# Last layer's experts: ranked by token count, sharing 128 columns in groups, with float32 weights unsplit

## The chip, the cores and the metric

The kernel runs on one core of a Trainium2 chip, as one launch. The metric is the time of one execution in device microseconds (us), median of the runs; less is better.

## The reference

Two transformer blocks in float32 run one after the other. The first block has two layers; each is a mixer (layer 0: Fourier mixing with neighbourhood attention; layer 1: retention) followed by a mixture of 16 experts of which each token takes two. Layer 0's experts see 512 tokens, layer 1's only the 256 latent tokens. The change touches the experts of layer 1 alone, whose weights are three matrices per expert: `w1` and `w3` of 1024x512, `w2` of 512x1024, 6 MB in float32 for each expert.

```python
def moe_ffn(tok, router_w, router_b, w1, w3, w2):
    T = tok.shape[0]
    scores = jax.nn.sigmoid((tok @ router_w).astype(jnp.float32))
...
    gate = jnp.sum(jax.nn.one_hot(expert_idx, N_EXPERTS, dtype=jnp.float32) * w[..., None], axis=1).astype(tok.dtype)
    out = jnp.zeros_like(tok)
    for e in range(N_EXPERTS):
        hid = jax.nn.silu(tok @ w1[e]) * (tok @ w3[e])
        out = out + gate[:, e:e + 1] * (hid @ w2[e])
    return out
```

With the reference's inputs, layer 1's 16 experts get 13, 23, 17, 17, 73, 64, 44, 39, 23, 20, 20, 17, 33, 45, 40 and 24 tokens (512 places in all).

## The kernel before

The residual stream `hT` lies transposed on the chip. The order of work is the program order of each engine's queue, set by the Tile framework's scheduler from the order in the code, from pools of buffers and from the semaphores that they need.

The function `moe(l, ss)` serves both layers. It routes (statistics, sigmoid, first two experts of the best group; `posm`, L1013, is each token's place in its expert's list), writes the tokens' normed rows into `nat` in a high and a low f32r part (L534, L537), and then works expert by expert, each in 128 columns:

- `choose` (L1050) makes one-hot columns for a pair of experts, `gather` (L1074) multiplies `nat` with them to get the transposed rows `xe` of the pair, read out on ScalarE and VectorE (L1079, L1077).
- `product` takes a weight in units of 1 MB. `unit` loads one (L172, issued on SP's queue into one of six 8 KB-per-partition buffers, four row blocks of 512 columns, so 2 KB in one piece), ScalarE rounds it to a high part `wh` (L186), VectorE, or GpSimd for every fourth block pair, makes the low part `wl` (L189). `mm3` (L198, L199, L200) then multiplies three times, high by high, low by high and high by low, 128 rows by 512 columns each. An expert has 24 such steps, layer 1 so 16x24x3 = 1152 matmuls.
- The hidden rows are transposed on TensorE (L258), split, and multiplied with `w2`; the result is scaled by the gate into `y` (L1099 ScalarE, L1100 VectorE), and `scatter` (L1119, L1120) adds the rows back through a one-hot `back` (L1103) into four PSUM banks `acc`, 16 matmuls for each expert.
- After expert 1, `overflow` holds a branch (L1217) for experts with more than 128 tokens, which is not taken. After expert 3, `bias_setup` prepares the second block's biases, with one large copy on GpSimd's queue.

After the last scatter `residual` adds the sum to `hT`, `stat_chunk2` (L473, L475) takes the squares, and `second` (L1311 on) is the second block, whose first products need the norm of the new stream.

## Time and profile before

| | us |
|---|---|
| median of 3 runs | 1856.89 |
| lowest and highest | 1853.49, 1857.39 |
| span of the profiled execution | 1851.5 |
| TensorE busy in the span | 1763.2 (95%) |
| layer 1's expert products, first to end of last | 1064.35 to 1404.18 |

The span is from the first to the last instruction in one execution under the profiler, the median is of whole executions; the profiled execution's own time outside the span is not given, so the difference of 5.4 us is taken as what lies around a span. In the second part of the page each digit is a fortieth of the span, 46.3 us; layer 1's experts are slices 23 to 30 (counted from 0).

### The profile page before, as it was taken

To read this page: it belongs to the slowest core of one execution; us is meant where nothing else is said; L and a number is where in the kernel's file an instruction comes from. 1 tells how busy PE (TensorE), PEld (TensorE's weight loads), DVE (VectorE), ACT (ScalarE), POOL (GpSimd) and SP (SyncE) were. 2 spreads that over 40 slices of the span, in tenths; PEclk is the share of its full clock that TensorE was granted. 3 is DMA by queue.
4 is the path that set the end of the run, shared out by engine and by line. 5 is a ranking of instruction groups with operands and counts; after the bars stand their busy time and mean duration, and the time that the engine had idled before them with its cause. 6 is when DMAs were issued, how large, how long until landed. Compare 5 with 4: busy or idle time off the path is not lost. (4 is left out here: it accounts for less than half of the span.)

```text
span 1851.5 us, 29457 instructions
## 1 busy us (share of the span) xinstructions
PE 1763.2 (95%) x11672; PEld 1500.9 (81%) x11672; DVE 1264.1 (68%) x1890; ACT 1002.0 (54%) x1388; POOL 492.7 (27%) x325
## 2 busy tenths in 40 slices
PE   6999999999999998999999899999998999999999
PEld 3766657777788876988999788888887989999989
DVE  6565553868888787654554587888887676577765
ACT  3343332656666665443343477777776455555543
POOL 2222102234444442220120243333333110122310
PEclk8999999999999998999999899999998999999999
DMA  9536544589888888355335279888885544543451
GB/s 315 140 111 198 185 144 182 199 277 293 283 284 290 293 290 301 115 205 183 117 113 194 80 262 332 294 307 309 291 285 159 166 143 152 188 133 119 137 190 39
DMA packets 249178, 384.13 MB, mean 207 GB/s; under 512 B 24273, under 2 KB 141074, under 8 KB 243850
## 3 DMA queue, kind: packets, MB, share of 16 engines
q1 hardware_dynamic: 245546, 373.71, 60.4%
q0 software_dynamic: 2608, 7.08, 1.9%
q8 instruction: 95, 1.56, 0.4%
q10 hardware_dynamic: 880, 1.38, 0.2%
q14 instruction: 49, 0.40, 0.1%
HBM read 375.19 MB, written 12.75 MB: 210 GB/s over the span
## 5 line engine op out<-in xcount | busy, mean ns | idle before, releaser
L189 DVE TENSOR_TENSOR wl<-w,wh 128x1024 fp32r<-128x1024 f32 x494 | 658.4, 1349 | 228.1 <-ACT wh L186 223.6
L186 ACT ACTIVATE wh<-w 128x1024 fp32r<-128x1024 f32 x592 | 621.5, 1059 | 343.4 <-PE ps L200 218.2
L189 POOL TENSOR_TENSOR wl<-w,wh 128x1024 fp32r<-128x1024 f32 x98 | 258.3, 2636 | 372.0 <-ACT wh L186 362.1
L199 PE MATMUL ps<-wl,xe 128*128 128x512 f32 x512 | 203.2, 397 | 13.5 <-POOL wl L189 13.0
L198 PE MATMUL ps<-wh,xe 128*128 128x512 f32 x512 | 203.7, 398 | 3.5 <-PEq L1217 3.5
L200 PE MATMUL ps<-wh,xe 128*128 128x512 f32 x512 | 201.8, 394 | 0.0
L198 PE MATMUL ps<-wh,xh 128*128 128x256 f32 x512 | 145.7, 285 | 1.1 <-DVE rt L799 0.7
L199 PE MATMUL ps<-wl,xh 128*128 128x256 f32 x512 | 143.7, 281 | 0.0
L200 PE MATMUL ps<-wh,xl 128*128 128x256 f32 x512 | 143.7, 281 | 0.0
L199 PEld LDWEIGHTS ps<-wl,xe 128*128 128x128 f32 x512 | 96.8, 189 | 39.7 <-POOL wl L189 20.1
L198 PEld LDWEIGHTS ps<-wh,xe 128*128 128x128 f32 x512 | 96.7, 189 | 23.6 <-issue 5.0
L200 PEld LDWEIGHTS ps<-wh,xe 128*128 128x128 f32 x512 | 96.6, 189 | 21.7 <-issue 0.8
L1074 PEld LDWEIGHTS ps<-oh,nat 128*128 128x128 f32 x768 | 104.3, 199 | 6.8 <-DVE oh L1050 1.2
L1074 PE MATMUL ps<-oh,nat 128*128 128x256 f32 x768 | 107.0, 291 | 0.8 <-DVE oh L1050 0.8
L199 PE MATMUL ps<-wl,hh 128*128 128x512 f32 x256 | 100.7, 393 | 2.2 <-DVE wl L189 2.2
L198 PE MATMUL ps<-wh,hh 128*128 128x512 f32 x256 | 101.0, 395 | 0.2 <-ACT xe L1079 0.2
L198 PE MATMUL ps<-x,wh 128*128 128x256 f32 x352 | 101.2, 288 | 0.0
L198 PEld LDWEIGHTS ps<-wh,xh 128*128 128x128 f32 x512 | 96.4, 188 | 5.4 <-issue 3.4
L200 PE MATMUL ps<-wh,hh 128*128 128x512 f32 x256 | 100.3, 392 | 0.0
L199 PE MATMUL ps<-x,wh 128*128 128x256 f32 x352 | 98.6, 280 | 0.0
L200 PE MATMUL ps<-x,wl 128*128 128x256 f32 x352 | 98.5, 280 | 0.0
L199 PEld LDWEIGHTS ps<-wl,xh 128*128 128x128 f32 x512 | 96.5, 188 | 0.1
(410 smaller groups left out, 4058.8 us busy)
## 6 DMA issues: line engine op xcount, KB each, us to landing
w<-in_moe_w_dram SPq DMA_DIRECT2D x192, 1024.0 KB, 6.0
w<-in_w_in_dram SPq DMA_DIRECT2D x48, 1024.0 KB, 5.5
w<-in_ada_w_dram SPq DMA_DIRECT2D x32, 1024.0 KB, 5.0
w<-in_ret_w_in_dram SPq DMA_DIRECT2D x24, 1024.0 KB, 5.4
w<-in_mixab_w_in_dram SPq DMA_DIRECT2D x10, 1024.0 KB, 6.0
w<-in_ada_w_dram SPq DMA_DIRECT2D x16, 512.0 KB, 8.8
ada<-in_ada_w_dram SPq DMA_DIRECT2D x8, 1024.0 KB, 9.0
w<-in_ret_w_out_dram SPq DMA_DIRECT2D x8, 1024.0 KB, 7.7
```

The lines of the kernel that those rows point to most:

```text
L186: nc.scalar.activation(hi, t[:, b:b + hk], AF.Copy)
L189: eng.tensor_tensor(out=lo, in0=t[:, b:b + hk], in1=hi.bitcast(F32), op=OP.subtract)
L198: mm(ps, lh, rh, start=start, stop=False, skip_group_check=skip)
L199: mm(ps, lh, rl, start=False, stop=False, skip_group_check=skip)
L200: mm(ps, ll, rh, start=False, stop=stop, skip_group_check=skip)
L1074: nc.tensor.matmul(ps[:, j], nat[part][:, t, k * P:(k + 1) * P], oh[:, t], start=t == 0, stop=t == NT - 1)
```

## The change

Layer 0 keeps `moe`, with its routing moved into `route`. Layer 1 gets `moe_late`. There, expert 15 is a group alone, and the other 15 are ranked by their token count on VectorE and GpSimd, after which they share 128 columns: the largest with one of the smallest, in nine groups (rank and columns below). The order of the ranks goes as integers to SP, which reads one before a group's loads and uses it in their addresses. A tile of 8 KB per partition holds 1 MB of a weight, now with 8 KB in one piece, since partition p takes rows 8p to 8p+7 (4p to 4p+3 in `w2`); `nat` and the hidden rows are written in the same spread order. The weights are multiplied as float32, unsplit, with float32 tokens; each expert's weights pass only the columns of its tokens: tiles of 32 columns in a group of 96 and 32, of 64 in a group of two 64s. Eight buffers for loads come on top of the standing three, in the room of the split weights' pool, which is released for the stage. The branch for overflow now tests whether any expert has more tokens than its columns.

```diff
+GROUPS = (((15, 128),), ((0, 96), (14, 32)), ((1, 96), (13, 32)), ((2, 64), (12, 64)), ((3, 64), (11, 64)),
+          ((4, 64), (10, 64)), ((5, 64), (9, 64)), ((6, 64), (8, 64)), ((7, 128),))
+CAPS = [dict(x for g in GROUPS for x in g)[r] for r in range(16)]
...
+            order = {}
+
+            def load(name, r, u, n, c):
+
+                w = I[name][l]
+                w = w[15:16] if r == 15 else w[bass.ds(order[r], 1)]
+                m = 2048 // c
+                return self.raw((P, m, c), w.rearrange("o (p k) c -> p (o k) c", k=n)[:, u * m:u * m + m, :])
+
+            def loads(g):
+
+                rs = [r for r, _ in GROUPS[g]]
+                return [[load(name, r, u, n, c) for r in rs]
+                        for name, n, c in (("moe_w1", 8, 512), ("moe_w3", 8, 512), ("moe_w2", 4, 1024)) for u in range(2)]
+
+            first = loads(0)
+            tl, places, gates, rows, nat = self.route(l, ss, rp, True)
...
+            b2 = lambda a, i: a.unsqueeze(i).to_broadcast([P, 16, 16])
+            key = tl([16])
+            V.scalar_tensor_tensor(out=key, in0=pos[:, 4, :], scalar=16.0, in1=self.down16, op0=OP.mult, op1=OP.add)
+            V.memset(key[:, 15:16], -1.0)
+            ge, up = tl([16, 16]), tl([16])
+            V.tensor_tensor(out=ge, in0=b2(key, 2), in1=b2(key, 1), op=OP.is_ge)
+            V.tensor_reduce(out=up, in_=ge, axis=AX.X, op=OP.add)
+
+            pm = tl([16, 16])
+            V.tensor_tensor(out=pm, in0=b2(up, 1), in1=b2(self.down16, 2), op=OP.is_equal)
+            V.tensor_tensor(out=ge, in0=pm, in1=b2(self.down16, 1), op=OP.mult)
+            V.tensor_reduce(out=up, in_=ge, axis=AX.X, op=OP.add)
+            oi = tl([16], I32, "order")
+            V.tensor_scalar(out=oi, in0=up, scalar1=-1.0, scalar2=16.0, op0=OP.mult, op1=OP.add)
+
+            def ranked(dst, x, eng):
+
+                t = tl([NT, 16, 16])
+                b4 = lambda a, i: a.unsqueeze(i).to_broadcast([P, NT, 16, 16])
+                eng.tensor_tensor(out=t, in0=b4(x, 2), in1=b4(pm, 1), op=OP.mult)
+                V.tensor_reduce(out=dst, in_=t, axis=AX.X, op=OP.add)
+
+            place = tl([NT, 16])
+            ranked(place, posm, V)
...
+            def choose(gs):
+
+                oh = wp.tile([P, NT, 256], F32R, tag="oh", name=self.name("oh"))
+                for t in range(NT):
+                    a = 0
+                    for g in gs:
+                        for r, n in GROUPS[g]:
+                            V.tensor_scalar(out=oh[:, t, a:a + n], in0=self.iota1[:, 0:n], scalar1=place[:, t, r:r + 1],
+                                            scalar2=None, op0=OP.is_equal)
+                            a += n
...
+            def gather(x, oh, w, c):
+
+                ps = self.psum((P, 2, 256))
+                for j in range(2):
+                    k = 2 * c + j
+                    for i in range(2 * NT):
+                        nc.tensor.matmul(ps[:, j, 0:w], nat[i % 2][:, i // 2, k * P:(k + 1) * P], oh[:, i // 2, 0:w],
+                                         start=i == 0, stop=i == 2 * NT - 1)
+                if c % 2:
+                    V.tensor_copy(x[:, 2 * c:2 * c + 2, 0:w], ps[:, :, 0:w])
+                else:
+                    nc.scalar.activation(x[:, 2 * c:2 * c + 2, 0:w], ps[:, :, 0:w], AF.Copy)
+
+            def columns(g):
+
+                ns = [n for _, n in GROUPS[g]]
+                w = min(min(ns), 128)
+                ends = np.cumsum(ns)
+                return [(a, a + w, int(np.searchsorted(ends, a, side="right"))) for a in range(0, P, w)]
+
+            def products(outs, lhs, ws, g):
+
+                m = ws[0][0].shape[1]
+                for u, we in enumerate(ws):
+                    for k in range(m):
+                        for c, ps in enumerate(outs):
+                            for a, b, e in columns(g):
+                                nc.tensor.matmul(ps[a:b], lhs(u * m + k)[:, a:b], we[e][:, k, 512 * c:512 * c + 512],
+                                                 start=u == k == 0, stop=u == len(ws) - 1 and k == m - 1)
+
+            def scatter(y, back, start, stop):
+                for k in range(KC):
+                    for i in range(2):
+                        nc.tensor.matmul(acc[k // 2][:, k % 2], y[i][:, k * P:(k + 1) * P], back,
+                                         start=start and k % 2 == i == 0, stop=stop and i == 1, skip_group_check=True)
+
+            def batch(gs):
+                oh, w = choose(gs)
+                return wp.tile([P, KC, 256], F32, tag="xe", name=self.name("xe")), oh, w
+
+
+            batches = [[0]] + [list(range(a, min(a + 2, NG))) for a in range(1, NG, 2)]
+            cur = batch(batches[0])
```

The loop over the groups, in the same order of steps as before, from the new file:

```diff
+            for bi, gs in enumerate(batches):
+                x, oh, _ = cur
+                nxt = batch(batches[bi + 1]) if bi + 1 < len(batches) else None
+                chunks = list(range(4)) if nxt else []
+                for i, g in enumerate(gs):
+                    if g:
+                        for r, _ in GROUPS[g]:
+                            order[r] = nc.values_load(oi[0:1, r:r + 1], engines=[mybir.EngineType.SP], min_val=0, max_val=15,
+                                                      skip_runtime_bounds_check_because="a place in a list of 16")
+                    ws = loads(g) if g else first
+                    xs = lambda k: x[:, k, P * i:P * i + P]
+                    h1 = self.psum()
+                    products([h1], xs, ws[0:2], g)
+                    hs = wp.tile([P, 512], F32, tag="hid", name=self.name("hid"))
+                    nc.scalar.activation(hs, h1, AF.Silu)
+                    if chunks:
+                        gather(*nxt, chunks.pop(0))
+                    h3 = self.psum()
+                    products([h3], xs, ws[2:4], g)
+
+                    hp = wp.tile([P, 4, P], F32, tag="hp", name=self.name("hp"))
+                    V.tensor_tensor(out=hp.rearrange("p k q -> p q k"), in0=hs.rearrange("p (q k) -> p q k", k=4),
+                                    in1=h3.rearrange("p (q k) -> p q k", k=4), op=OP.mult)
+                    if todo:
+                        scatter(*todo, g == 1, False)
+                    gate, back = slots(g, oh, P * i)
...
+                    tp = self.psum((P, 4, P))
+                    for j in range(4):
+                        self.T(tp[:, j, :], hp[:, j])
+                    hT = wp.tile([P, 4, P], F32, tag="hh", name=self.name("hh"))
+                    nc.scalar.activation(hT, tp, AF.Copy)
+                    while chunks and (len(gs) == 1 or len(chunks) > 2 * (1 - i)):
+                        gather(*nxt, chunks.pop(0))
+                    yp = [self.psum() for _ in range(2)]
+                    products(yp, lambda k: hT[:, k], ws[4:6], g)
+                    y = [wp.tile([P, D], F32R, tag=f"y{j}", name=self.name("y")) for j in range(2)]
+                    for c in range(2):
+                        s = slice(512 * c, 512 * c + 512)
+                        nc.scalar.activation(y[0][:, s], yp[c], AF.Copy, scale=gate)
+                        V.scalar_tensor_tensor(out=y[1][:, s], in0=yp[c], scalar=gate, in1=y[0][:, s].bitcast(F32),
+                                               op0=OP.mult, op1=OP.subtract)
+                    todo = y, back
+                    if g == 1:
+                        self.overflow(l, N, NT, cnt, 0, pk, wp, nat, acc, hs[:, 0:1])
+                    if g == 2:
+                        with self.tc.tile_pool(name="bias", bufs=1) as bp:
+                            self.bias_setup(bp)
```

`overflow`'s limit, its room, and the pool of the split weights:

```diff
-        ta = wp.tile([P, 2048], F32, tag="xe0", name=self.name("ova"))
-        tb = wp.tile([P, 2048], F32, tag="xe1", name=self.name("ovb"))
+        ta, tb = (self.raw((P, 2048), None) if l else wp.tile([P, 2048], F32, tag=f"xe{i}", name=self.name("ov"))
+                  for i in range(2))
         tw = self.raw((P, 4, 512), None)
...
-        with self.tc.If(reg > P):
+        with self.tc.If(reg > limit):
...
+        with k.splitting():
             ss = k.mixer0()
+            ss = k.moe(ss)
             ss = k.mixer1(ss)
+        ss = k.moe_late(ss)
+        with k.splitting():
+            k.second(ss)
```

On TensorE, before, in the middle of the last experts (`xe` are tokens' rows, `hh` hidden rows, `wh` and `wl` the weights' parts, `nat` the rows to gather from):

```order
L198 MATMUL ps_12840<-wh_12869,xe_12419 128x512
L199 MATMUL ps_12840<-wl_12870,xe_12419 128x512
L200 MATMUL ps_12840<-wh_12869,xe_12420 128x512
L1074 MATMUL ps_12886<-oh_12821,nat_10087 128x256 x4
L1074 MATMUL ps_12892<-oh_12821,nat_10088 128x256 x4
L198 MATMUL ps_12900<-wh_12903,hh_12746 128x512
L199 MATMUL ps_12900<-wl_12904,hh_12746 128x512
L200 MATMUL ps_12900<-wh_12903,hh_12747 128x512
```

Three matmuls make one step of one expert, on all 128 columns.

On TensorE, now, in a group of two experts of 64 columns (`w_11206` and `w_11210` are one expert's units of `w2`, `w_11208` the other's; the two `ps` are the two halves of the output):

```order
L1339 MATMUL ps_11299<-oh_11025,nat_10100 128x256
L1339 MATMUL ps_11299<-oh_11025,nat_10101 128x256
L1360 MATMUL ps_11309<-w_11206,hh_11297 64x512
L1360 MATMUL ps_11310<-w_11206,hh_11297 64x512
L1360 MATMUL ps_11309<-w_11208,hh_11297 64x512
L1360 MATMUL ps_11310<-w_11208,hh_11297 64x512
L1360 MATMUL ps_11309<-w_11206,hh_11297 64x512
L1360 MATMUL ps_11309<-w_11208,hh_11297 64x512
L1360 MATMUL ps_11310<-w_11206,hh_11297 64x512
L1360 MATMUL ps_11310<-w_11208,hh_11297 64x512
```

One matmul of each expert makes a step of both, each on 64 columns. In the first four rows of a unit of `w2`, two matmuls of the same expert stand one behind the other.

On SP, at the start of layer 1, before (`w` are weights' buffers):

```order
L172 DMA w_10264<-in_moe_w_dram 128x4x512
L172 DMA w_9885<-in_ret_w_out_dram 128x8x256
L172 DMA w_10405<-in_moe_w_dram 128x4x512
L172 DMA w_9955<-in_ret_w_out_dram 128x8x256
L172 DMA w_10307<-in_moe_w_dram 128x4x512
L172 DMA w_10329<-in_moe_w_dram 128x4x512
```

And now:

```order
L182 DMA w_10041<-in_moe_w_dram 128x2048
L182 DMA w_10043<-in_moe_w_dram 128x2048
L1388 TENSOR_LOAD order_10121
L182 ISA
L182 DMA w_10390<-in_moe_w_dram 128x2048
L1388 TENSOR_LOAD order_10121
L182 ISA
L182 DMA w_10392<-in_moe_w_dram 128x2048
L182 ISA
```

The six loads of expert 15 stand ahead as before, then SP reads `order` from the chip ahead of each rank's first load; the loads behind it, with an address that is worked out (ISA), wait for it.

On SP, around the overflow branch, before:

```order
L1216 TENSOR_LOAD cnti_10585
L1216 ISA x2
L172 DMA w_10718<-in_moe_w_dram 128x4x512
L172 DMA w_10740<-in_moe_w_dram 128x4x512
L172 DMA w_10783<-in_moe_w_dram 128x4x512
L172 DMA w_10805<-in_moe_w_dram 128x4x512
L172 DMA w_10843<-in_moe_w_dram 128x4x512
L172 DMA w_10921<-in_moe_w_dram 128x4x512
L1217 COMPARE_AND_BRANCH
```

And now:

```order
L182 ISA
L182 DMA w_10408<-in_moe_w_dram 128x2048
L1459 TENSOR_LOAD cnti_10583
L1459 ISA x2
L182 ISA
L182 DMA w_10410<-in_moe_w_dram 128x2048
L182 ISA
L182 DMA w_10412<-in_moe_w_dram 128x2048
L1461 COMPARE_AND_BRANCH
```

Two loads stand between the read of the count and the branch, where six stood; all loads of group 2 and later come behind the branch.

## Rows read from the trace of the kernel before

**Rows 1.** The page's part 2, forty slices: TensorE's clock and the DMA engines' busy tenths.

```profile
PEclk8999999999999998999999899999998999999999
...
DMA  9536544589888888355335279888885544543451
```

**Rows 2.** Busy time by stretch: us, engines' busy, granted clock, DMA share, GB/s.

```profile
705.00:712.00 7.00, 7.00 (x50) 6.41 (x49) 7.00 (x14) 1.74 (x2) 3.30 (x1) 1.00 1.01 421
...
1100.00:1400.00 300.00, 294.87 (x1521) 247.92 (x1520) 248.28 (x267) 218.14 (x248) 106.90 (x45) 1.00 0.86 299
...
1064.00:1404.00 340.00, 334.44 (x1723) 281.22 (x1722) 283.20 (x313) 247.94 (x282) 121.59 (x50) 1.00 0.85 292
```

**Rows 3.** SP's own waits from 1064 to 1404 us: total, times, longest.

```profile
SPq L172 <- DVE wl L189: 178.5, 89, 32.6
...
SPq L172 <- POOL wl L189: 131.0, 45, 3.5
...
SPq L1217 <- SPq L1217: 6.6, 4, 2.7
```

**Rows 4.** Groups by line and shape, 1064 to 1404 us: busy us, mean ns, idle before.

```profile
L186 ACT ACTIVATE wh<-w 128x1024 fp32r<-128x1024 f32 x189 | 198.7, 1060 | 74.0 <-PE ps L200 73.9
...
L189 DVE TENSOR_TENSOR wl<-w,wh 128x1024 fp32r<-128x1024 f32 x143 | 192.3, 1373 | 42.5 <-ACT wh L186 39.3
...
L1100 DVE SCALAR_TENSOR_TENSOR y<-ps,r,y 128x512 fp32r<-128x512 f32 x31 | 23.0, 741 | 3.5 <-ACT y L1099 3.5
...
L1099 ACT ACTIVATE y<-ps,r 128x512 fp32r<-128x512 f32 x31 | 21.4, 689 | 11.5 <-PE ps L200 9.8
...
L1141 DVE TENSOR_TENSOR hid<-hid,ps 128x512 f32<-128x512 f32 x16 | 10.8, 675 | 0.0
```

**Rows 5.** TensorE's timeline in layer 1's experts: start, us, line, operation.

```profile
1064.35 0.40 PE L198 MATMUL ps<-wh,xe 128*128 128x512 f32 x1
...
1379.69 0.39 PE L198 MATMUL ps<-wh,xe 128*128 128x512 f32 x1
...
1381.05 0.39 PE L198 MATMUL ps<-wh,xe 128*128 128x512 f32 x1
...
1404.18 0.28 PE L1119 MATMUL ps<-back,y 128*128 128x256 f32 x1
...
1404.29 0.28 PE L1120 MATMUL ps<-back,y 128*128 128x256 f32 x1
...
1418.43 0.58 PE L198 MATMUL ps<-wh,xp 128*128 128x256 f32 x1 [1.72 <-ACT xp L1327]
```

**Rows 6.** VectorE's timeline in layer 1's routing.

```profile
1055.74 0.42 DVE L537 TENSOR_TENSOR nat<-ps,nat 128x256 fp32r<-128x256 f32 x1
...
1056.09 0.19 DVE L1013 SCALAR_TENSOR_TENSOR r<-ps,r 128x32 f32<-128x32 f32 x1
```

**Rows 7.** SP's timeline: the issue of one load.

```profile
1000.30 0.37 SPq L172 DMA_DIRECT2D w<-in_moe_w_dram  x1
```

**Rows 8.** One line, L390, its matmuls: ns min/median/max, first and last start.

```profile
L390 PE MATMUL ps<-w,silu_c x256: 592/593/617, 135.7 to 923.4; 128*32 128x512 f32 x128
```

**Rows 9.** TensorE's timeline elsewhere: 64-column tiles, after the first branch, 32-column tiles.

```profile
134.12 1.68 PE L663 MATMUL ps<-PT,v 128*64 128x256 f32 x14
...
392.34 0.76 PE L198 MATMUL ps<-wh,xe 128*128 128x512 f32 x1 [3.51 <-PEq L1217]
...
721.97 1.92 PE L390 MATMUL ps<-w,silu_c 128*32 128x512 f32 x16
```

**Rows 10.** One line, L1217, the branch: ns min/median/max, first and last start.

```profile
L1217 PEldq COMPARE_BRANCH  x2: 328/2192/4057, 388.1 to 1100.7; - x2
...
L1217 SPq EVENT_SEMAPHORE  x16: 17/17/17, 391.8 to 1105.0; - x16
```

**Rows 11.** The page's part 6: DMA issues, KB each, median us from issue to landing.

```profile
w<-in_moe_w_dram SPq DMA_DIRECT2D x192, 1024.0 KB, 6.0
...
w<-in_ada_w_dram SPq DMA_DIRECT2D x32, 1024.0 KB, 5.0
```

More of the change, by code (lines that the diff above doesn't have):

```diff
@@ new lines, in rows, with moe @@
+                self.fill(NF[k])
+        return tl, places, gates, rows, nat
+    def moe(self, ss):
+        nc, I, V = self.nc, self.I, self.nc.vector
+        l, n0, NT, N = 0, 0, 4, 512
+        with ExitStack() as es:
+            op = lambda n, b=1: es.enter_context(self.tc.tile_pool(name=f"{n}{l}", bufs=b))
+            rp, wp = op("route"), op("moe", 2)
+            es.enter_context(self.buffers(2))
+            self.aside.append(self.ada(1, 0, lambda i: wp.tile([P, 2048], F32, tag=f"xe{i % 2}", name=self.name("ada"))))
+            self.fill(2)
+            tl, places, gates, rows, nat = self.route(l, ss, rp, False)
+            rows()
+            pos, posm = places()
@@ L1198, in overflow @@
+    def overflow(self, l, N, NT, cnt, limit, pk, wp, nat, acc, after):
         nc, I, V = self.nc, self.I, self.nc.vector
```

321 lines of the change are left out of this document (164 added, 157 removed).

## Prediction

> **What bounds the kernel now.** I read the page's slices first. Layer 1's experts are slices 23 to 30; in slices 24 to 29 the DMA engines are busy eight or nine tenths, at a clock of nine tenths or more but in one slice [rows 1], so either TensorE or the transfers could set the pace. The table by stretch decides: from 1100 to 1400 us TensorE is busy 294.87 of 300 us at a clock of 1.00, and the DMA engines move 299 GB/s at a share of 0.86 [rows 2]. TensorE is the bound. That the DMA engines are not is seen in SP's waits: 178.5 and 131.0 us of the 340 it stood waiting for a buffer that VectorE or GpSimd had not finished splitting [rows 3]. The splits fill ScalarE for 198.7 us and VectorE for 192.3 us [rows 4] beside TensorE's work. Then the timeline of TensorE: six matmuls from 1379.69 to 1381.05, so 0.227 us each and 0.68 us for a step of three [rows 5]. Sixteen experts of 24 steps are 384 x 0.68 = 261 us of the 339.8 between the first product at 1064.35 and the end of the last at 1404.18 [rows 5]; gathers, scatters, transposes and small waits are the rest. So the stage falls if TensorE has fewer or cheaper steps, until the transfers of 96 MB set the pace.
>
> **The change, part by part.**
>
> *The start.* Loads by rank need the order. Places stand at 1056.09 [rows 6]. By VectorE's order there come to the order's write nine operations of 128x256 (four of them `nat`'s) at 0.42 [rows 6], two of 128x512 at 0.675 [rows 4] and six small ones at 0.19 [rows 6]: 6.3 us, 1062.4. SP then reads a register and issues a load, 0.37 [rows 7] plus the read, which no row prices on SP: from 0.2 to 2 us, I take one. Ranked loads move from 1064. Expert 15's six loads are in before that. The first product needs `place` (same chain), two one-hots and 32 gathers of about 0.11: 1067.3, 3 us later than now.
>
> *TensorE's products.* Nine groups of 24 steps are 216 steps instead of 384. A step of four 32-column tiles has its form in ada's matmuls: 16 records are eight float32 matmuls of two records, in four sets of four tiles that start together; with 0.593 for one record [rows 8], (1.92 - 0.593)/3 = 0.44 from set to set [rows 9], two sets a step: 0.88 us. Tiles of 64 columns: seven pairs of records of 256 columns in 1.68 us [rows 9], at most 0.24 a set, so at most 0.96 for a step of 512. Groups of one expert pass the same 512 columns; no row has that shape, and I take the same. All: 216 x 0.88 = 190 us; with 0.96 it is 207, and that is the upper end for the two successive matmuls of one expert at each `w2` unit too (two steps in five groups, 9 us).
>
> *TensorE's other work.* A scatter matmul takes 0.115 [rows 5]. Nine groups of 16 scatters, 17 us (now 16 x 16, 29); 160 gathers, at most 18 (now 256); transposes and slots about 7. Waits that nothing covers: in each group the hidden product on VectorE (0.68) and the transposed copy (0.6 by ScalarE's 0.689 [rows 4]); between groups, `y` on ScalarE and VectorE, 0.69 and 0.74 [rows 4], before half of the scatters. 9 x 1.3 + 8 x 1.4 = 23 us. The branch on TensorE: 0.33 in layer 1 and 4.06 in layer 0 [rows 10], I take 1. **Sum for TensorE: 190 + 17 + 18 + 7 + 23 + 1 = 256, from 1067.3 to 1323.**
>
> *The splits* (189 on ScalarE [rows 4], as many on VectorE and GpSimd) go and cost nothing: they lay beside TensorE. What was waiting on them, SP's 309 us, goes to the next limit, the DMA engines.
>
> *The transfers.* 90 loads of 1.049 MB go by rank. Their pieces grow from 2 to 8 KB. The nearest row with 8 KB pieces (2048 float32 of a row) is the stretch of modulation weights: 421 GB/s at a share of 1.01 [rows 2], 2.5 us a load. A pair's 12 loads take 30 us, a little more than TensorE's 28 for a group; so from group 4 or so the loads lead. SP's queue also empties at the branch: it waited there 6.6 us in all [rows 3], its last semaphore at 1105.0 [rows 10]; now only two loads stand ahead of it, the room for the branch takes three of the eleven buffers till group 1 is done, and group 2's twelve loads come behind. I put 16 us to that and 4 to other transfers: an estimate, not less than 7 by rows 3. The last pair's loads end at 1064 + 84 x 2.5 + 20 = 1294; landing 2, its last four steps 3.5: 1299.5; then the last group, alone on TensorE, 24 x 0.88 + scatters 2 + waits 3 = 26: **1325**.
>
> The Trainium skill (DMA: Bandwidth & Descriptors, Specifications) gives a limit of some 358 GB/s for a core's reads from HBM. By it a load is 2.93 us and the same walk, without 10 us of losses that it hides, comes to about 1352. The stretch at 421 GB/s [rows 2] lies above that, though for only 7 us; so I go by the row.
>
> *Both together.* Both ways end at 1323 to 1325 and I take 1324 for the last product, 80 us before 1404.18. The tail grows by 1: both halves of `w2` end together, so `y` (0.7) is fully waited for and all 16 scatters come behind it. From there the stream's norm, 14 us to the second block's first product at 1418.43 [rows 5], covers the new split of its first weights (1.06 and 1.37 [rows 4]) though their room comes free only now. Net -79 of the span of 1851.5: 1772.5. The median stands 5.4 us above that span; so **1778 us**.
>
> **The rivals.**
>
> *The loads keep a lower rate.* For it: no row shows 421 GB/s for longer than 7 us, and 250 us must be kept up. Against: what held the rate at 299 was buffers [rows 2, 3], and there are eleven now for six. Halfway between, at 360 GB/s, a load is 2.9 us, the last pair ends at 1064 + 244 + 10, the products at 1350, the kernel at 1804. At 299 GB/s, 3.5 us a load, the last pair ends at 1064 + 295 + 10, the products at 1400, so 1854: no change. This is the rival that takes the gain. The Trainium skill's limit (DMA: Bandwidth & Descriptors, Specifications) would put it near the middle of these.
>
> *Loads with an address from a register are issued late.* If SP, for each of them, had to wait for something like a landing (5.0 to 6.0 us [rows 11]) in place of 0.37, the 90 loads would go one by one: 90 x 5 = 450, the products end near 1519 and the kernel at 1973: **slower**. It decides from (1404 - 1064 - 20)/90 = 3.5 us a load; under 2.5 it costs nothing. For it: no row has such a load in a long series. Against: nothing in the order makes SP wait for a landing, only for the address (ISA) and a buffer.
>
> *Column tiles take turns.* If tiles of different experts didn't overlap, two groups would have one turn, five two, and two four: 20 x 24 x 0.88 = 422 us in place of 190, the end at 1555, 2009 us: slower. Against: the sets of four and of two start together [rows 9]; for: there every tile's work comes from one line's even rhythm, here from two experts' loads.
>
> *It doesn't do what it says.* An expert above its columns would open the branch for all 16 experts, 16 x 2 x 6 loads one behind the other at 5 us and more, some 1000 us. The counts (73, 64, 45 ... in the reference's inputs; the largest allowed 96 and the next 96, then 64) and 24 for expert 15 speak against it: 1 in 100.
>
> *Half clock.* After 3.51 us of waiting the first matmul in layer 0 took 0.76 instead of 0.40 [rows 9]. If waits for loads do that in each of nine groups for some 4 us, 18 to 27 us are lost, most of it under the loads: end near 1335 to 1345, 1790 to 1800. It is inside my range.
>
> **How the numbers follow.** The forecast with its sizes: 0.70 (1750 to 1820). Its low end is TensorE without the 23 us of waits and 5 us of slack in the step, the end at 1296; its high end the loads at 340 GB/s (1366), or the step at 0.96 (+ 17) together with 27 us of half clock (1368). Lower rate of transfers, still faster, 1820 to 1853: 0.12. No change, within 0.2% (3.7 us, about what a measurement here can tell): 0.03. Slower: registers 0.05, turns 0.05, the branch and others 0.02: 0.12. Better than 1750: 0.03. So faster 0.85, same 0.03, slower 0.12. To hold 8 in 10, I take the range up to 1840: 1750 to 1840.
>
> **What would show it.** Right: in the changed profile the products' line has records near 0.593 us with four (or two) tiles starting together; the stage is some 257 us long at a clock of 1.00; no split stands in it; the DMA engines move over 400 GB/s at a share near 1 from about 1150 on, after a gap behind the branch; SP waits for products, not splits, and issues loads within a us. Wrong: GB/s near 300 to 360 with SP never waiting for a buffer (rate); loads 4 us or more apart on SP with idle DMA engines (registers); records of different tiles one behind another (turns); a clock below 0.9 in the stage (half clock); DMAs of the branch's body in the trace.

## The result and the profile after

The changed kernel takes 1790.41 us (median of four runs, 1786.78 to 1793.64), the kernel before took 1857.14 in the same comparison: a ratio of 0.9639, 95% interval 0.9621 to 0.9657. The forecast was 1778, the range 1750 to 1840.

The profiled execution after took 1791.71 us with a span of 1790.0. That of before was its fastest run, 1853.49, with a span of 1851.5. So about 2 us lie around a span in both; the rest of the 5.4 us that the forecast put there, 3.4, was the distance from that fastest run to the median.

The page's part 2, after (before: [rows 1]); layer 1's experts are now slices 23 to 29:

```profile
PEclk8999999899999999899999979999998999999999
DMA  9635552669888889545542447999965544533360
GB/s 315 156 109 174 186 183 97 258 226 310 289 289 284 292 286 339 170 158 172 165 142 94 150 175 263 398 420 421 421 242 150 172 144 151 187 119 118 119 212 24
```

Four slices stand at 398 to 421 GB/s, where slices of the same work before moved 299 [rows 2]. One slice, number 23 counted from 0, has a clock of seven tenths. The table by stretch, after, shows where the stage changes its limit (columns as in [rows 2]):

```profile
1073.50:1100.60 27.10, 26.93 (x91) 14.11 (x93) 4.61 (x18) 3.30 (x6) 0.00 (x0) 0.94 0.80 277
1100.60:1126.70 26.10, 26.06 (x233) 10.65 (x232) 5.18 (x18) 3.17 (x5) 0.00 (x0) 1.00 0.77 284
1126.70:1168.30 41.60, 34.99 (x247) 14.49 (x247) 8.26 (x25) 3.85 (x6) 0.57 (x1) 0.92 1.00 406
1168.30:1285.20 116.90, 111.01 (x545) 48.46 (x544) 17.86 (x46) 12.67 (x20) 0.55 (x1) 1.00 1.01 420
1285.20:1315.00 29.80, 27.58 (x122) 10.70 (x122) 3.55 (x9) 2.57 (x4) 0.00 (x0) 0.94 1.01 417
```

From 1168 to 1285 us TensorE is busy for 111.01 of 116.90 us at full clock (2.4 GHz), and the DMA engines at a share of 1.01: neither has much room left. VectorE and ScalarE, which had been busy for over 80% and 70% of such a stretch, mostly with splits, are down to 15% and 11%. The Trainium skill (DMA: Bandwidth & Descriptors, Specifications) gives some 358 GB/s as a core's limit for HBM, half of a stack's 716; the 420 GB/s kept up for 117 us here are above that.

SP's waits from 1064 to 1340 us, after:

```profile
SPq L182 <- PE ps L1360: 181.9, 63, 11.9
...
SPq L1388 <- DVE order L1253: 17.1, 1, 17.1
SPq L1461 <- SPq L1461: 4.6, 3, 3.1
SPq L182 <- PEq L1461: 4.1, 1, 4.1
```

The waits for a split [rows 3] are gone; SP waits for products to give a buffer back. SP's issue of the ranked loads, one line's instructions (columns as in [rows 10]):

```profile
L182 SPq FUSED_REGOPS  x90: 46/46/61, 1065.4 to 1299.0; - x90
L182 SPq MOVE w<-in_moe_w_dram x90: 29/29/42, 1065.5 to 1299.1; - x90
L182 SPq DMA_DIRECT2D w<-in_moe_w_dram x90: 332/333/1033, 1065.6 to 1301.2; - x90
```

A load with an address from a register costs SP 0.33 us and two short instructions. TensorE's groups by shape in the stage, after:

```profile
L1360 PE MATMUL ps<-w,xe 128*64 128x512 f32 x320 | 76.2, 596 | 0.0
L1360 PE MATMUL ps<-w,hh 128*64 128x512 f32 x160 | 37.4, 620 | 0.7 <-ACT hh L1413 0.7
L1360 PE MATMUL ps<-w,xe 128*32 128x512 f32 x256 | 30.2, 605 | 0.0
L1360 PE MATMUL ps<-w,xe 128*128 128x512 f32 x64 | 29.5, 619 | 0.0
```

One record is 0.6 us in every shape; how many stand side by side shows in the timeline. TensorE's timeline, after (start, us, operation, wait before it):

```profile
1066.64 7.06 PE L1339 MATMUL ps<-oh,nat 128*128 128x128 f32 x32 [6.01 <-DVE oh L1303]
1073.50 8.61 PE L1360 MATMUL ps<-w,xe 128*128 128x512 f32 x16
...
1082.89 7.03 PE L1360 MATMUL ps<-w,xe 128*128 128x512 f32 x16
...
1119.59 7.07 PE L1360 MATMUL ps<-w,hh 128*32 128x512 f32 x64
1131.83 3.75 PE L1366 MATMUL ps<-back,y 128*128 128x256 f32 x16 [5.17 <-PEq L1461]
...
1138.79 7.07 PE L1360 MATMUL ps<-w,xe 128*32 128x512 f32 x64
...
1168.29 1.07 PE L1360 MATMUL ps<-w,xe 128*64 128x512 f32 x2
...
1187.21 0.66 PE L268 MATMUL ps<-c_main,hp 128*128 128x128 f32 x4 [1.19 <-DVE hp L1402]
...
1188.74 7.14 PE L1360 MATMUL ps<-w,hh 128*64 128x512 f32 x32
...
1197.52 1.07 PE L1360 MATMUL ps<-w,xe 128*64 128x512 f32 x2
...
1304.58 8.83 PE L1360 MATMUL ps<-w,hh 128*64 128x512 f32 x32 [0.75 <-ACT hh L1413]
...
1331.52 7.13 PE L1360 MATMUL ps<-w,hh 128*128 128x512 f32 x16 [0.75 <-ACT hh L1413]
...
1351.45 0.58 PE L208 MATMUL ps<-wh,xp 128*128 128x256 f32 x1 [1.72 <-ACT xp L1570]
```

Eight steps take 7.03 us with 16 records on 128 columns, 7.07 with 64 records on four tiles, 7.14 with 32 records on two: 0.88 us a step in every shape, so the tiles run side by side. A group of two experts repeats every 29.2 us (1168.29, 1197.52), with no wait for a load anywhere.

Measured from the last write of the stream before the stage (VectorE, 1043.26 before, 1046.52 after), the first product comes at 21.1 us before and 27.0 after, and the second block's first product at 375.2 and 304.9. So the stage gave 70.2 us. Outside it, 3.3 us were lost ahead of the stage and 5.5 behind (1851.5 - 1418.43 = 433.1 before, 1790.0 - 1351.45 = 438.6 after): 61.5 us net in the span. The 3.3 us ahead are no more than two executions of one kernel differ by: in a second profile of the kernel before (below) that last write stands at 1046.95.

### The profile page after: what moved, and what is told of

The parts are those of the page before. It is cut to its first block, busy times and chain, and to the rows that moved or that the text cites. A ratio compares the mean times of both kernels' runs of the same rounds, so it can differ in the third digit from the quotient of the medians.

```text
span 1790.0 us, 28059 instructions
## 1 busy us (share of the span) xinstructions
PE 1684.6 (94%) x11244; PEld 1337.9 (75%) x11244; DVE 1031.9 (58%) x1717; ACT 778.8 (44%) x1146; POOL 375.4 (21%) x282
## 5 line engine op out<-in xcount | busy, mean ns | idle before, releaser
L199 DVE TENSOR_TENSOR wl<-w,wh 128x1024 fp32r<-128x1024 f32 x350 | 469.4, 1353 | 188.6 <-ACT wh L196 187.3
L196 ACT ACTIVATE wh<-w 128x1024 fp32r<-128x1024 f32 x400 | 419.6, 1058 | 279.9 <-PE ps L210 145.1
L199 POOL TENSOR_TENSOR wl<-w,wh 128x1024 fp32r<-128x1024 f32 x50 | 137.9, 2758 | 160.4 <-ACT wh L196 160.4
L1360 PE MATMUL ps<-w,xe 128*64 128x512 f32 (+2 forms) x640 | 135.9, 602 | 0.0
L209 PE MATMUL ps<-wl,xe 128*128 128x512 f32 x256 | 102.5, 400 | 13.3 <-POOL wl L199 13.3
L208 PE MATMUL ps<-wh,xe 128*128 128x512 f32 x256 | 102.4, 400 | 3.1 <-PEq L1461 3.1
L210 PE MATMUL ps<-wh,xe 128*128 128x512 f32 x256 | 101.2, 395 | 0.0
L210 PEld LDWEIGHTS ps<-wh,xl 128*128 128x128 f32 x512 | 98.1, 192 | 0.0
L208 PE MATMUL ps<-xh,wh 128*128 128x512 f32 (+1 forms) x224 | 82.7, 381 | 2.4 <-ACT xh L534 2.1
L209 PE MATMUL ps<-xl,wh 128*128 128x512 f32 (+1 forms) x224 | 82.3, 369 | 0.3 <-DVE xl L535 0.3
L210 PE MATMUL ps<-xh,wl 128*128 128x512 f32 (+1 forms) x224 | 81.2, 365 | 0.0
```

The source lines that it names most:

```text
L196: nc.scalar.activation(hi, t[:, b:b + hk], AF.Copy)
L199: eng.tensor_tensor(out=lo, in0=t[:, b:b + hk], in1=hi.bitcast(F32), op=OP.subtract)
L208: mm(ps, lh, rh, start=start, stop=False, skip_group_check=skip)
L209: mm(ps, lh, rl, start=False, stop=False, skip_group_check=skip)
L210: mm(ps, ll, rh, start=False, stop=stop, skip_group_check=skip)
L1360: nc.tensor.matmul(ps[a:b], lhs(u * m + k)[:, a:b], we[e][:, k, 512 * c:512 * c + 512], start=u == k == 0, stop=u == len(ws) - 1 and k == ...
```

## The experiments

**Expert 15's columns ahead of the ranking.** Group 0 needs no rank, so its one-hot columns can come from `posm` directly.

```diff
+            oh0 = wp.tile([P, NT, 256], F32R, tag="oh", name=self.name("oh"))
+            for t in range(NT):
+                V.tensor_scalar(out=oh0[:, t, 0:P], in0=self.iota1[:, 0:P], scalar1=posm[:, t, 15:16], scalar2=None,
+                                op0=OP.is_equal)
...
             def choose(gs):
+                if gs == [0]:
+                    return oh0, P
```

> The one-hot columns of expert 15 (the first group, which needs no rank) are made from its own places, before the ranking, so that its gather does not wait for the ranking on VectorE. Theory (TensorE sat idle 6.0 us before that gather and then ran it and the first steps at the half clock, 7.06 us for 32 matmuls and 8.61 for eight steps in place of about 3.7 and 7.03): the first product starts at about 1066 to 1068 in place of 1073.5, at full clock, and the whole is 5 to 9 us faster than the changed kernel. Rival (the loads set the pace, and they start with the ranking as before, at 1065): the first group is early, the later ones wait for loads, and the whole gains under 2 us.

1782.96 us, ratio 0.9604 [0.9591, 0.9617]. The first product comes 22.5 us after the stream's last write instead of 27.0. The clock did not come along; its timeline:

```profile
1060.31 6.45 PE L1345 MATMUL ps<-oh,nat 128*128 128x128 f32 x29 [0.55 <-DVE nat L548]
1066.56 9.11 PE L1366 MATMUL ps<-w,xe 128*128 128x512 f32 x16
```

The wait of 6 us is gone, but 29 gathers still take 6.45 us, 0.22 each, about twice what later gathers of 256 columns take at full clock (after, 16 in 2.13 us), and the first eight steps 9.11. So the wait that had been blamed for the low clock is not its cause. The low clock is not new either. In the kernel before, the granted clock stood at 0.50 from 1048 to 1060 us, from the routing's small matmuls into the first gathers, with TensorE busy for 7.66 of 12 us (columns as in [rows 2]), and the first 32 gathers took 0.21 us each as well:

```profile
1048.00:1060.00 12.00, 7.66 (x33) 4.88 (x33) 10.50 (x42) 9.19 (x20) 5.49 (x8) 0.50 0.00 0
```

```profile
1057.83 6.69 PE L1074 MATMUL ps<-oh,nat 128*128 128x256 f32 x32 [0.82 <-DVE oh L1050]
```

**A shorter body behind the branch.** In layer 1 the overflow body holds two blocks after the change, one before. Here it holds one again (the first 128 tokens of an overflowing expert are left out, a path that these inputs don't take).

```diff
-                for b in range(0 if l else 1, NT):
+                for b in range(1, NT):
```

> The body of the overflow branch (not taken here) is made for one block of 128 instead of two; what it leaves out is the first block of an overflowing expert. Theory (TensorE's branch instruction took 6.96 us in the changed kernel and 0.33 before, with 118 against 64 of its instructions jumped over: it is the length of the jump): the branch instruction on TensorE falls below 1 us, the wait of 5.2 us and the half clock behind it go, and the whole is 5 to 9 us faster than the changed kernel. Rival (the branch waits for SP's loads to land or for the semaphores of the other engines): the wait stays within 1 us of 5.2 and the time is the same.

1784.20 us, ratio 0.9614 [0.9601, 0.9627]. The branch on TensorE's queue, after and then with the short body. Each row holds two branches, layer 0's and layer 1's; after, TensorE's queue goes on at 1131.6 us, so the long one, from 1124.6, is layer 1's; with the short body layer 1's is the short one.

```profile
L1461 PEldq COMPARE_BRANCH  x2: 3622/5290/6957, 388.1 to 1124.6; - x2
```

```profile
L1461 PEldq COMPARE_BRANCH  x2: 1601/2509/3417, 389.0 to 1123.7; - x2
```

6.96 us have become 1.60, and in the timeline TensorE's wait of 5.17 us became 0.35, with full clock behind it:

```profile
1126.20 2.32 PE L1366 MATMUL ps<-back,y 128*128 128x256 f32 x16 [0.35 <-PEq L1461]
```

From the end of group 1's last product to the first full row of group 2's `w1`, 12.1 us became 5.9. In the kernel before, the same branch took 0.33 [rows 10].

The length of the body is not all of it. With the two blocks left as they are, layer 1's branch took 3.69 us in the run with a sixth of the loads left out and 3.73 in the run without sharing (both below), where 35 and 46 GB/s moved during the branch, against 381 after. The traces' DMA packets show what goes along with the wait. Instructions arrive on a queue of their own, q8, in transfers of 16 KB; TensorE executes some 250 instructions between two of them, so the queue is taken to be TensorE's. It has one transfer from 1129.0 to 1130.2 us after, inside the long branch, and one from 1122.9 to 1124.0 with the short body, at the start of the short one (packets, MB, share of the DMA engines in that window):

```profile
q8 instruction: 1, 0.02, 5.0%
```

```profile
q8 instruction: 1, 0.02, 5.9%
```

After, this transfer begins 4.57 us behind the branch's start, and the branch ends 1.43 us behind the transfer's end. With the short body it begins 0.82 us ahead of the branch, which again ends 1.39 us behind its end. The same 1.3 to 1.5 us stand at both branches in all traces of this case, but for layer 1's in the three profiles with the old experts: those took 0.33 us, and the last such transfer had ended over 12 us before. In the two runs with little traffic the transfer begins 1.0 us behind the branch's start; in the others with two blocks it begins 3.6 to 4.6 us behind, while 371 to 423 GB/s move. So, as far as these traces show, TensorE stood at the branch until instructions had arrived, and they came later where the loads filled the DMA engines. Why a shorter body has them on their way earlier is not shown.

**Row blocks as before.** The loads in four or eight row blocks, pieces of 2 and 4 KB in place of 8, and `nat` and the hidden rows unspread.

```diff
-                return self.raw((P, m, c), w.rearrange("o (p k) c -> p (o k) c", k=n)[:, u * m:u * m + m, :])
+                return self.raw((P, m, c), w.rearrange("o (k p) c -> p (o k) c", p=P)[:, u * m:u * m + m, :])
...
-            tl, places, gates, rows, nat = self.route(l, ss, rp, True)
+            tl, places, gates, rows, nat = self.route(l, ss, rp, False)
...
```

> Weights are loaded by row blocks as before the change (2 KB pieces for the first two matrices, 4 KB for the third), and the tokens' and hidden rows are in plain order. Theory (the 8 KB pieces lift the loads to 421 GB/s, where they just keep up with a pair's 29.2 us on TensorE): GB/s in the steady stretch falls to 380 to 400, a pair takes 31.5 to 33 us, TensorE waits for loads, and the whole is 10 to 25 us slower than the changed kernel. Rival (TensorE alone sets the pace, loads have room): same time, within 3 us.

1793.67 us, ratio 0.9662 [0.9643, 0.9681], against 0.9639 [0.9621, 0.9657] with large pieces: the intervals overlap. The trace tells more. One stretch, and TensorE's wait for loads in the stage:

```profile
1168.00:1285.00 117.00, 110.17 (x534) 47.45 (x532) 16.51 (x46) 12.07 (x19) 0.00 (x0) 1.00 1.04 394
```

```profile
PE ps L1360 <- DMA w<-in_moe_w_dram: 5.2, 5, 1.6
```

Small pieces bring 394 GB/s where large ones bring 420, and TensorE waits for loads from 1261 us on. So large pieces are worth 6% of the rate, and only 5 us of waits, since 394 almost does. The rate was as expected, the time was not: until the waits begin, a group takes 28.9 us (1163.77 to 1192.66), 0.3 less than after, since TensorE waits 0.85 us for the hidden product in plain order and 1.19 for the spread one.

**The kernel before, once more.** Unchanged, to see whether the 8 us outside the stage belong to the execution.

> The kernel before, unchanged, for a second profile. In the changed kernel's profile the 256-column f32r matmuls outside the stage start 0.120 us apart, in the one of before 0.116 to 0.117, some 9 us in all over parts that the change does not touch. If that is from run to run, a second profile of before can show 0.120 too and its span is then near 1858 to 1862; if it belongs to the change, 0.116 to 0.117 again and a span near 1851 to 1854.

1858.58 us, one run. Its span of 1856.8 is longer than expected, as the stream's last write before the stage comes 3.7 us later than in the first profile (1046.95); from the second block's first product to the end it takes 434.3 us, against 433.1. The matmuls outside the stage keep the rhythm that they had in [rows 5]'s execution. Here it is in the second block, from TensorE's timeline before, a stretch of equal rows of which each is one matmul:

```profile
1600.05 0.28 PE L198 MATMUL ps<-x,wh 128*128 128x256 f32 x1
...
1601.10 0.28 PE L198 MATMUL ps<-x,wh 128*128 128x256 f32 x1
```

and after:

```profile
1538.22 0.28 PE L208 MATMUL ps<-x,wh 128*128 128x256 f32 x1
...
1539.66 0.28 PE L208 MATMUL ps<-x,wh 128*128 128x256 f32 x1
```

Nine matmuls in 1.05 us, 0.117 each, against twelve in 1.44, 0.120. The repeat shows 0.116 to 0.117 again.

**The kernel before with its pools in the new order.** The change takes the split weights' pool last, so that it can be released for the stage. The same order in the kernel before:

```diff
-        self.wh = ctx.enter_context(tc.tile_pool(name="wsplit", bufs=4))
         self.sm = ctx.enter_context(tc.tile_pool(name="small", bufs=3))
...
         ctx.enter_context(self.buffers(RAW))
+        self.wh = ctx.enter_context(tc.tile_pool(name="wsplit", bufs=4))
```

> The kernel before, with only the pool of the split weights taken after the standing buffers, as the changed kernel has to take it, so that the split weights lie at other addresses (the first at 73536 in place of 40480 bytes); nothing else differs. In the changed kernel and in three variants of it the 256-column f32r matmuls of the untouched parts start 0.120 us apart, in both profiles of the kernel before 0.116 to 0.117. Theory (the changed place of the split weights makes it): 0.120 here too, and the whole 5 to 10 us slower than before. Rival (it is the tokens' side, the order of routing, or the code): 0.116 to 0.117 and the same time as before.

1865.51 us, ratio 1.0043 [1.0028, 1.0058]: 8 us slower by nothing but places in memory. The rhythm is 0.120, as the theory had it. The weight loads of the second block, before and then with the new order (busy us, mean ns):

```profile
L199 PEld LDWEIGHTS ps<-x,wh 128*128 128x128 f32 x352 | 66.2, 188 | 1.1 <-issue 0.2
```

```profile
L199 PEld LDWEIGHTS ps<-x,wh 128*128 128x128 f32 x352 | 67.2, 191 | 1.2 <-issue 0.2
```

But most of these 8 us lie in the stage itself, which the changed kernel replaces. From the stream's last write to the second block's first product it takes 382.0 us, against 375.2 and 375.5 in the two profiles of the kernel before; from there to the end 437.9, against 433.1 and 434.3. In layer 1's experts a step of three matmuls now takes 0.70 us instead of 0.68 [rows 5]:

```profile
1199.82 0.40 PE L198 MATMUL ps<-wh,xe 128*128 128x512 f32 x1
...
1200.52 0.39 PE L198 MATMUL ps<-wh,xe 128*128 128x512 f32 x1
```

**Padding by 64 and by 32 bytes.** An unused tile ahead of the pools in the changed kernel shifts all that follows.

```diff
+        cp.tile([P, 16], F32, name="pad")
```

(`[P, 8]` for 32 bytes.)

> The changed kernel with 64 bytes per partition left empty ahead of the routing's constants, so that all that lies behind moves by 64 bytes; no instruction differs. Theory (an address's low bits make the 0.120 us: the tokens' parts of the products lie at 128 bytes past a multiple of 256 where they lay at 64 before): back at 64 past a multiple of 128 the spacing is 0.116 to 0.117 again, 5 to 9 us faster than the changed kernel. Rival (the region of the split weights, or nothing that 64 bytes change): 0.120 still and the same time as the changed kernel.

> The same with 32 bytes left empty, so that the split weights lie 32 bytes past a multiple of 128 as before, and the tokens' parts too. If the low bits of the split weights' address make the 0.120 us, the spacing is 0.116 to 0.117 here and not with 64 bytes; if neither, 0.120 in both.

1786.26 us, ratio 0.962 [0.960, 0.964], and 1784.12 in one run. The rhythm stays at 0.120 in both, so the low bits of the address are not it. The two serve as controls too: with no edit in the stage, it took 300.7 and 300.5 us (from the stream's last write to the second block's first product), 4 less than the 304.9 of the changed kernel's profile. There the last group of two ran its `w2` steps in 8.83 us at a clock of 0.83, here in 7.14, and the branch's wait was 4.57 and 4.37 instead of 5.17. Differences of 4 us between the medians of these kernels therefore say little; what the two edits above gain is read from the rows of the start and of the branch. By the same measure the stage took 299.1 us with expert 15's own columns and 298.0 with the short body, so against these controls only some 1.5 and 2.7 us of the two gains reach the stage's end.

**A sixth of the loads left out.** Of each `w2` only the first half is loaded, and used twice (the second half is left out).

```diff
+                      for u in range(1 if name == "moe_w2" else 2)]
+                return ws + ws[4:5]
```

> The second half of each expert's third matrix is not loaded and its first half is used twice: five loads for six, 75 by rank in place of 90; TensorE does all its steps. What it leaves out is that half of the matrix. Theory (TensorE sets the pace of the steady groups, 29.2 us a pair; the loads just keep up): a pair still takes 29.2 us within 0.3, the DMA share falls to about 0.85 in the steady stretch, and the whole is within 4 us of the changed kernel. Rival (the loads set the pace): a pair falls to about 25 us, and the whole is 20 to 30 us faster.

1784.46 us, one run. With the DMA engines at a share of 0.93 the groups come every 29.8 us, no sooner than with all loads, and TensorE waits for no load in the stage:

```profile
1168.00:1285.00 117.00, 112.24 (x543) 48.35 (x544) 17.85 (x46) 12.45 (x20) 0.00 (x0) 1.00 0.93 372
```

So transfers do not set the pace. The share is above the 0.85 expected and the group 0.6 us longer than 29.2, beyond the 0.3 allowed: here scatters and gathers stand in more pieces between the products, which may be the reason but is not shown to be.

**Both edits together.** Expert 15's own columns, and the overflow body once, in a loop of two turns, so that nothing is left out.

```diff
+                for b in range(0 if l else 1, 1 if l else NT):
+                    with self.tc.For_i(0, NT, 1) if l else ExitStack():
...
```

> The changed kernel with two edits together: expert 15's one-hot columns are made from the places as they stand, ahead of the ranking, and the overflow body stands once, in a loop of two turns, so that it is still there in full and the jump over it on TensorE is half as long. Theory (the two losses are separate: one lies in the wait for the ranking at the start, 6.5 us, the other in the jump and the half clock behind it, 4.6 us): the gains add, 9 to 12 us below the changed kernel, 1778 to 1782, the branch's wait on TensorE under 4 us as with the short body, no wait of TensorE for a load. Rival (the loads take up what TensorE gains, since they move at 420 GB/s with 29.9 us for a pair against TensorE's 29.2): only the larger of the two gains stands, 1783 to 1785, and waits for loads stand on TensorE.

1783.46 us, ratio 0.9599 [0.9578, 0.962]: not told apart from either edit alone. The start gained as in the first experiment (22.7 us to the first product). At the branch the jump was short again, yet a new gap followed:

```profile
1121.24 2.20 PE L1372 MATMUL ps<-back,y 128*128 128x256 f32 x15 [0.35 <-PEq L1467]
1125.82 0.37 PE L1372 MATMUL ps<-back,y 128*128 128x256 f32 x1 [2.37 <-issue]
```

The timeline names nothing that TensorE waited for in the 2.37 us, but again a transfer on q8 lies in them (1123.60 to 1124.56 us), and the matmul starts 1.26 us behind its end. The passage took 8.7 us, between the 12.1 and the 5.9, and the stage 297.6. Neither theory was right in full: the gains do not add, but no wait for loads took them.

**Sixteen groups of one.** The sharing alone undone; ranking, layout and unsplit float32 stay.

```diff
+GROUPS = (((15, 128),),) + tuple(((r, 128),) for r in range(15))
```

> The changed kernel with sixteen groups of one expert each, 128 columns, ranked as before and in float32 unsplit: the grouping alone is undone. Theory (the gain is the sharing of columns; a float32 step of 512 columns costs 0.88 us whether one expert or four tiles use it): 384 steps of 0.88 are 338 us in place of 190, with 7 more groups' scatters, transposes and waits of some 4 us each, so 150 to 185 us more than the changed kernel, 1940 to 1975, slower than the kernel before by about 100, the DMA engines near 240 GB/s. Rival (float32 unsplit is by itself worth something, since the kernel before spent three f32r matmuls of 0.227 us, 0.68, on a step): then the steps of one expert are cheaper than 0.68 us, and the time lies at or below 1857.

1933.48 us, one run: 143 above the changed kernel and 76 above the kernel before, 7 under the range expected. Its timeline has the same 7.03 us for eight steps, now of one expert:

```profile
1205.70 7.03 PE L1359 MATMUL ps<-w,xe 128*128 128x512 f32 x16
```

An unsplit step costs 0.88 us where three f32r matmuls cost 0.68 [rows 5]. So unsplit weights by themselves lose; the sharing is what pays.

**A third of TensorE's steps left out.** The second half of the rows of each unit of `w1` and `w3` is left out of the products; all loads stay.

```diff
-                    for k in range(m):
+                    for k in range(m if len(outs) == 2 else m // 2):
...
```

> The changed kernel with the second half of the rows of each unit of w1 and w3 left out of the products (8 of 24 steps of a group), while all loads stay. TensorE's time for a pair of groups falls from 29.2 by 14 to about 15 us. Theory (transfers stand only just behind TensorE: twelve loads at 420 GB/s take 29.9 us): pairs still take 29 to 30 us where the loads stand at a share of 1, TensorE waits for loads, and the kernel falls only by what the stretch up to 1168 us had lost at the loads' expense, 5 to 20 us, to 1770 to 1785, in place of the 63 us that 72 steps of 0.88 would give. Rival (the loads could go faster, if buffers came free sooner): pairs of 20 us or less, over 500 GB/s, the kernel near 1730.

1766.90 us, one run, 23.5 below the changed kernel instead of the 63 that 72 steps would be, and 3 below the range expected. (The 14 and 15 us of the expectation are a slip: eight steps are 7 us of a group, so TensorE alone would need 22.) The steady groups begin at 1172.29 and 1202.10, and TensorE's wait for loads in the stage is no longer nothing:

```profile
1172.29 1.07 PE L1360 MATMUL ps<-w,xe 128*64 128x512 f32 x2
...
1202.10 1.07 PE L1360 MATMUL ps<-w,xe 128*64 128x512 f32 x2
```

```profile
PE ps L1360 <- DMA w<-in_moe_w_dram: 17.4, 20, 1.5
```

Now loads set the pace, at 421 GB/s and 29.8 us a group; the gain came ahead of these groups, where the DMA engines had had room (from the first product to the first group with tiles of 64 columns, 71.9 us instead of 94.8). That is the floor of the steady groups, and the changed kernel's 29.2 stand on it: from 1168 to 1285 us TensorE consumed 48 loads, while 420 GB/s brought about 47 (49.1 of 50.3 MB), so the lead shrank by one.

**The split weights low again.** The first experiment's kernel with the standing buffers given back and taken anew around the stage, so that the split weights lie ahead of them.

```diff
...
-        with k.splitting():
+        with k.splitting(), k.buffers(RAW):
...
-        ss = k.moe_late(ss)
-        with k.splitting():
+        with k.buffers(RAW):
+            ss = k.moe_late(ss)
+        with k.splitting(), k.buffers(RAW):
```

> The kernel of e1_own_place with the split weights' pool taken ahead of the three standing buffers again, as in the kernel before (the first high part at 49,024 bytes of a partition, in place of 73,600; before 40,480), for which the standing buffers are given back and taken anew around the stage. Theory (the place of the split weights cost the blocks outside the stage some 8 us): the spacing of the 256-column f32r matmuls is 0.116 to 0.117 us again in both blocks, the part behind the second block's first product is 433 us long as in the kernel before, not 438, and the kernel takes 1775 to 1779. Rival (it is one particular place that is good, or the place relative to another buffer, not the lower region): the spacing stays at 0.120, and the time at 1783. In both, expert 15's loads and the second block's first load can no longer start before the pools change hands, for which up to 3 us may be lost at either end of the stage.

1786.17 us, ratio 0.9624 [0.9605, 0.9644], rhythm 0.120: a miss. Neither the lower half of the memory as such nor the standing buffers' place (now where they were before, but for 64 bytes) brings the 0.117 back. What is left is the exact place of the split weights, 40,480, or that of the small tiles, which moved with them; the two were not told apart.

## Why the prediction was right, and where its steps were off

The sign and the mechanism held: the time lies in the range, 12.4 us above the forecast. By its steps, in the spans (1772.5 forecast, 1790.0 measured, 17.5 apart):

- **The step of 0.88 us** was right (0.879), in all three shapes, with the two successive matmuls of one expert in `w2` at no price (7.14 against 7.03). The upper end of 0.96 was not needed. "Column tiles take turns" falls with the same rows.
- **The start**, forecast 3 us later than before, came 5.9 later, counted from the stream's last write. The ranking was quicker than forecast; the 32 gathers took 7.06 us at half clock (1.2 GHz) instead of 3.5. Failing term: the gathers at full clock, 2.9 us net. The trace of the kernel before already had its first 32 gathers at half clock (6.69 us), which the forecast did not read.
- **The branch, "I take 1"**, failed: the jump took 6.96 us and TensorE waited 5.17 for it, with a clock of 0.66 from 1130 to 1140 us; together 6.3 us more than in the kernel with the short body. The rows gave 0.33 and 4.06 as bounds [rows 10]; the change lengthened layer 1's body from one block to two, which the sum did not count, and even the upper bound was too low: in the traces the branch ends 1.43 us behind a transfer of instructions, which came 4.57 us into the branch with the loads at 381 GB/s and 1.0 us in with little traffic.
- **Half clock** cost 1.6 us in the first eight steps and 1.7 in the last group of two: far less than the 18 to 27 us of that rival, and not behind waits for loads. With the branch that makes 9.6 us; the products took 265.1 us from first to last where TensorE's sum had 255.7.
- **The transfers**: 421 GB/s was right, now over 117 us instead of 7, so the lower-rate rival fell. "From group 4 or so the loads lead" was not: TensorE leads by a little, 29.2 us a group, and 29.8 is what the loads alone allow. Leaving out loads brought no shorter group, and leaving out steps brought no more than the loads allow. Both walks ended within 2 us of each other in the forecast, so the mistake cost nothing.
- **The tail**, forecast 1 us longer, was 1.4 shorter (12.8 us against 14.25).
- **"The second block unaffected"** failed by 5.5 us. Most of that is the change's: the new order of the pools alone made this part of the kernel before 3.6 to 4.8 us longer, and in all eleven profiles of the changed kernel and its variants it takes 438 us or more. That term stood nowhere in the sum. For the 3.3 us ahead of the stage no cause is shown; the kernel before repeated came 3.7 later by itself.
- **Registers**: loads late by their address fell; 0.33 us an issue. The overflow body was not run.
- **A misreading without effect**: slices 24 to 29 are all at nine tenths of the clock [rows 1]; the slice at eight tenths is number 30.

Sum of the misses: 3.3 + 2.9 + 8.4 (products, against the 256.7 between the forecast's 1067.3 and 1324) - 2.4 + 5.5 = 17.7, against 17.5 measured. The median came only 12.4 above the forecast because 5.4 had been added for what lies around a span, where 1.7 does, and because the profiled execution was 1.3 above the median; that part is luck.

The sign rests on the sharing: without it the kernel stands at 1933, with it at 1790.

## What to carry to other kernels

A multiplication that costs more per step can still win if it lets several small problems share one pass: here 0.88 us for two experts beat twice 0.68 for the split form. Before a stage's compute is cut further, work out where its transfers stand; this one has both within 2% of each other, and 7 us taken from each group's products left its steady groups as long as they were. When a pool is moved to make room, time the untouched kernel with only that move: places alone cost the kernel before 8 us here, most of it in a stage that the change then replaced. And read the clock of a stage's first matmuls from the trace of before: half clock at the start stood there already.

## What was not expected of the hardware

- A branch whose body is skipped can cost TensorE several us: in layer 1 0.33 before, 6.96 after, 6.00 with expert 15's own columns, 1.60 with the body halved, 3.7 with the full body but little DMA traffic. Layer 0's took 3.4 to 4.7 in these kernels, with a body that no edit touched. Where it took longer than 0.33 us, it ended 1.3 to 1.5 us behind a 16 KB transfer of instructions.
- The order of the pools changed the rhythm of 256-column f32r matmuls from 0.117 to 0.120 us and their weight loads from 188 to 191 ns, and in the kernel before that of 512-column ones in layer 1's experts from 0.227 to 0.234; shifts of 32 and 64 bytes and a move of the split weights to 49,024 did not change it back.
- TensorE's clock stood at 0.50 during the first gathers (1060 to 1070 us after, 1060 to 1067 with both edits) also where the wait of 6 us ahead of them had been taken away. It had fallen in the routing, in the kernel before too. The last group of two ran at 0.83 in some kernels and at full clock in others, after the same waits of 1.19 and 0.75 us; what decides this stays open.
